# Decoder trunk (gated linear attention layer, then S5 layer): v projections of two heads issued one head earlier, gate chains of the next head issued early, q/k ahead of the output transposes

## The chip, the cores and the metric

One core of a Trainium2 chip. The metric is the device time of one execution in microseconds; the time of the kernel before is the median of three runs.

## What is computed

A sequence of 512 tokens of width 1024 goes through two layers and a final RMSNorm. The change lies in the first, gated linear attention (GLA):

```python
h = rmsnorm(x, gla_norm)
q, k, v, z, r = split(h @ w_in)                 # q, k: 4 heads x 128; v, z: 4 heads x 512; r: 16
log_a = log_sigmoid(r @ w_gate_up + b_gate) / 16
# per head, in chunks: bcum = cumsum(log_a) in the chunk
att = tril((q * exp(bcum)) @ (k * exp(-bcum)).T)
o   = att @ v + (q * exp(bcum)) @ state         # state: decayed sum of k_end.T @ v over chunks before
o   = rmsnorm_per_head(o) * head_gain * silu(z)
x   = x + o @ w_out
```

The second layer is an S5 state space layer (`u` and `z` projections, a grouped complex-diagonal scan, a GLU with a 2048x2048 matrix, an output projection). Its tables (powers of the diagonal, products with B and C) depend on parameters alone. This kernel computes them beside the first layer.

## The kernel before, in words

**Matmuls.** Every dense product is made of three fp32r matmuls (`three`, L194): high times high, high times low, low times high. A weight unit (`wunit`, L178) is one 512 KB DMA from the SP queue, a cast on ScalarE (ACT, L161) for the high part and a subtraction on VectorE (DVE, L162) for the low part. For `w_out` the unit is scaled, in two halves, on ACT (L164) and DVE (L165). A projection for one head (`dense_tok`, L204) takes four such units. It adds into four PSUM tiles of the pool `pd`, which has four in all, one for each 128 tokens; they come free when the projection's evacuation has read them. With `late` the evacuation of the last unit comes after the generator's last yield.

**A head** (loop at L634). `gate(h)` (L425): a small matmul (L427) into a tile of the pool `pt` (two tiles), then a chain of ACT and DVE operations (L429 to L451) that ends in the factors `eq` and `ek`. `proj_qk` (L454): two weight units into two `po` tiles, evacuated by multiplying with `eq` and `ek` (L465, L466). `ptrn(0..3)`: the transposes (`turn`, L399, L406) of the gated output of the head before, each into a `pt` tile. Then `weave` (L541) walks through a list of projections and, at each yield ("slot"), issues the attention pieces whose position in `POS` is that slot: `scores` (c, L485, a `pt` tile), `state` (s, L499) and `mix` (x, L515) of the four 128-token blocks. `proj_v` (L381) evacuates v into eight `big` tiles (L164, L165), which s and x read. `proj_z` (L389) evacuates z into the gate of the head's output (L393, L394, L396) and needs the norm that ends with x3. `proj_out(h - 1)` (L534) adds the product of the head before with `w_out` to x (L537).

The slots before: head 0 has z only (4 slots), since its v is made ahead of the loop; heads 1 and 2 have v, out of the head before, z (12 slots); head 3 has v, half of out, z (10 slots) and then the other half of out beside its own transposes.

**S5 tables.** `tick` issues the six parts of `small` (L968), some 200 small DVE and GpSimd (POOL) operations with a round trip through DRAM; its fourth part and its fifth use `pt` tiles for transposes (L1179, L1192; L1222, evacuated by L1224). After that `hook` issues steps of a plan: F (`compute`, L1282, on POOL, and `finish_b`, L1318), Z (`finish_z`, L1323, with eight matmuls L1330 into a `pt` tile), E (`etab`, L1247, the first three on DVE, the others on POOL). Each hook adds `RATES[head]` (0.84 in heads 1 and 2, 0.88 in head 3) to a counter, and each whole number issues a step. Before, hooks begin in head 1: two after q/k (`QZ[0]`) and one a slot.

**Order.** The order that instructions are issued in gives each a priority; `later(n)` moves a block behind by n (attention pieces by `SCP` = -20, so ahead; `small` by `LOW1` = 20). The framework's planner then orders each engine's queue by priority and by what it expects to be ready, so a projection can stand ahead of pieces that were issued before it but wait. Each engine works through its queue in that order.

```python
        if h == 0:
            weave([z], tk)
            prep.zero()
            tick()
        elif h < NH - 1:
            weave([proj_v(h, *v), proj_out(h - 1, prev, range(2)), z], tk)
```

Of the kernel before, what the change touches and what calls it, by code (L numbers as in the profile page):

```python
# [24 lines left out]
NT = SEQ // P  # L25
DI = 2048
NH = 4
# [21 lines left out]
SU = 11  # L49
SS = 22  # L50
SE = 3
WR, WH, Q4, BIG = 2, 5, 9, 28
TOFF = 5
SMALL = [0, 1, 3, 4, 5]
NPRE = 3
TS = [2, 3, 3, 3, 4, 5, 5, 5, 6, 6, 7, 8, 10, 10, 11, 12]
# [3 lines left out]
SCP = -20  # L60
USP = 50
SEQ0 = 'h0 u h2 u h4 u s h6 u x0 t x1 q0 q1 t'
GP = 4
RATES = [0.84, 0.84, 0.88, 0.94, 0.94]
LOWS = {'F': 0, 'Z': 20, 'E': 100, 'G': 0}
ETABS = [2, 3, 3, 3, 3, 3, 3, 3, 4, 4, 4, 4, 4, 4, 4, 7, 8]
POS = [[0, 0, 1, 2, 1, 2, 3, 1, 2, 3, 3], [0, 1, 1, 3, 4, 5, 6, 5, 5, 7, 9], [0, 1, 3, 4, 4, 5, 6, 5, 6, 8, 8], [1,
    1, 4, 4, 4, 5, 6, 6, 6, 6, 8], [0, 0, 0, 0]]
A0S = [3, 4, 5, 6, 7, 8, 9, 10, 11, 12, 13, 14, 15, 16, 17, 18]
SRS = [2, 3, 4, 5, 6, 7, 8, 9, 10, 11, 12, 13, 14, 15, 16, 17]  # L70
# [5 lines left out]
LBS = [0, 0, 0, 6, 7, 7, 8, 9, 10, 11, 12, 13, 14, 15, 16, 18]  # L76
UNITP = [0, 1, 0, 1, 1, 1, 0, 1, 1, 1, 0, 1, 1, 0, 1, 1, 1, 1, 1, 0, 0, 1, 1, 1, 1, 1, 0, 1, 0, 0, 1, 0, 0, 0, 0, 0,
    0, 0, 1, 1]
TORD = ['c0 c1 s0 c2 x0 s1 x1 c3 s2 x2 x3', 'c0 c1 c2 c3 x0 s0 s1 x1 s2 x2 x3', 'c0 c1 c2 c3 s0 x0 s1 s2 x1 x2 x3',
    'c0 c1 c2 c3 s0 s1 x0 x1 s2 x2 x3']  # L80
PACE = [2, 2, 2, 2, 2, 2, 3, 1, 2, 2, 2, 2, 2, 2, 2, 2, 2, 2, 1, 1, 1, 1]
QZ = [2, 3]
GPOS = [0, 0, 7]


def f(t):
# [4 lines left out]
def trunk_kernel(  # L91
# [5 lines left out]
    nc = tc.nc  # L97
# [20 lines left out]
    def PT():  # L118
        return PS_("pt", 2)
# [10 lines left out]
    def q2(dt=F32, n=512):  # L130
        return T_([P, n], "q2", 8, dt)

    def big(dt=F32):
        return T_([P, 512], "big", BIG, dt)
# [4 lines left out]
    def tmp(dt=F32):  # L139
        return T_([P, 512], "tmp", 4, dt)  # L140
# [18 lines left out]
    def split(dst_hi, dst_lo, src, scale=None, E=V):  # L159
        if scale is None:  # L160
            i0 = A.copy(out=dst_hi, in_=src)  # L161
            i1 = E.tensor_tensor(out=dst_lo, in0=src, in1=f(dst_hi), op=SUB)  # L162
        else:
            i0 = A.activation(out=dst_hi, in_=src, func=AF.Copy, scale=scale)  # L164
            i1 = V.scalar_tensor_tensor(out=dst_lo, in0=src, scalar=scale, in1=f(dst_hi), op0=MUL, op1=SUB)  # L165
        return i0.ins, i1.ins
# [214 lines left out]
    def proj_v(h, vh, vl):  # L381
        vh += [big(F32R) for _ in range(NT)]
        vl += [big(F32R) for _ in range(NT)]

        def ev(tb, acc):
            split(vh[tb], vl[tb], acc, scale=rs1[:, tb:tb + 1])
        return dense_tok(w_v[h], hh, hl, ev)
# [11 lines left out]
    def turn(box, out_):  # L399
        oh, ol = out_  # L400

        def fn(tb):
            o2 = box[0][tb]
            pt = PT()
            for k in range(4):
                PE.transpose(pt[:, k * P:(k + 1) * P], o2[:, k * P:(k + 1) * P], ident)  # L406
            oh.append(q2(F32R))
            ol.append(q2(F32R))
            split(oh[tb], ol[tb], pt)
        return fn  # L410
# [14 lines left out]
    def gate(h):  # L425
        lg = PT()
        PE.matmul(lg, lhsT=wg[:, h * P:(h + 1) * P], rhs=rT, start=True, stop=True)  # L427
        mn = tmp()
        V.tensor_scalar(out=mn, in0=lg, scalar1=bg[:, h:h + 1], scalar2=0.0, op0=ADD, op1=ALU.min)  # L429
        ab = tmp()  # L430
        A.activation(out=ab, in_=lg, func=AF.Abs, bias=bg[:, h:h + 1])
        A.activation(out=ab, in_=ab, func=AF.Exp, scale=-1.0)
        A.activation(out=ab, in_=ab, func=AF.Ln, bias=1.0)
        V.tensor_tensor(out=mn, in0=mn, in1=ab, op=SUB)
        be = tmp().rearrange("p (b c) -> p b c", b=NT)
        V.tensor_tensor_scan(out=be.rearrange("p b c -> p (b c)"), data0=seg.rearrange("p b c -> p (b c)"),
                             data1=mn, initial=0.0, op0=MUL, op1=ADD)
        sm = T_([P, 3, NT], "gsm", 2)
        V.tensor_copy(out=sm[:, 0, :], in_=be[:, :, 63])
        V.tensor_copy(out=sm[:, 1, :], in_=be[:, :, 127])  # L440
        V.tensor_tensor(out=sm[:, 2, :], in0=sm[:, 1, :], in1=sm[:, 0, :], op=SUB)
        V.tensor_tensor(out=be, in0=be, in1=sm[:, 0, :].unsqueeze(2).to_broadcast([P, NT, P]), op=SUB)
        es = T_([P, 3, NT], "ges", 2)
        A.activation(out=es, in_=sm, func=AF.Exp, scale=1.0 / 16)
        eq = big()
        ek = big()
        b2 = be.rearrange("p b c -> p (b c)")
        A.activation(out=eq, in_=b2, func=AF.Exp, scale=1.0 / 16)
        A.activation(out=ek, in_=b2, func=AF.Exp, scale=-1.0 / 16)
        V.tensor_tensor(out=eq, in0=eq, in1=rbc, op=MUL)  # L450
        V.tensor_tensor(out=ek, in0=ek, in1=rbc, op=MUL)  # L451
        return es, eq, ek
# [81 lines left out]
    def proj_out(h, o, ns):  # L534
        for n in ns:
            def ev(tb, acc, n=n):
                V.tensor_tensor(out=xts[tb][n], in0=acc, in1=xts[tb][n], op=ADD)  # L537
            yield from dense_tok(w_out[h, n], o[0], o[1], ev, per_tb=True,
                                 scales=[hgp[:, k:k + 1] for k in range(4)])

    def weave(gens, toks):  # L541
        i = 0
        for gen in gens:
            for _ in gen:
                with later(SCP):
                    for p, fn, b in toks:
                        if p == i:
                            fn(b)
                if prep.t < TOFF:
                    if i % 2:  # L550
                        tick()
                else:
                    hook()
                i += 1

    def toks(h, at_):
        fns = {"c": at_.scores, "s": at_.state, "x": at_.mix}
        off = {"c": 0, "s": 4, "x": 7}
        return [(POS[h][off[t[0]] + int(t[1])], fns[t[0]], int(t[1])) for t in TORD[h].split()]

# [37 lines left out]
    v0 = ([], [])  # L598
# [32 lines left out]

    prev = ptrn = None
    nxt = []
    for h in range(NH):  # L634
        v = ([], [])
        box = []
        o = ([], [])
        trn = turn(box, o)
        if h == 0:
            v = v0  # L640
            proj_r()
        phase[0] = h - 1 if h else 0
        gt = nxt.pop() if nxt else gate(h)
        if h > 0:
            ptrn(0)
            ptrn(1)
        qk = proj_qk(h, gt[1], gt[2])
        if h > 0:
            ptrn(2)
            ptrn(3)  # L650
        if h == 0:
            tick()
        else:
            for _ in range(QZ[0]):
                hook()
        at_ = Attn(gt[0], qk, v, box)
        z = proj_z(h, box)
        tk = toks(h, at_)
        if h < 3 and GP >> h & 1:
            tk.append((GPOS[h], lambda b: nxt.append(gate(b)), h + 1))  # L660
        if h == 0:
            weave([z], tk)
            prep.zero()
            tick()
        elif h < NH - 1:
            weave([proj_v(h, *v), proj_out(h - 1, prev, range(2)), z], tk)
        else:
            weave([proj_v(h, *v), proj_out(h - 1, prev, range(1)), z], tk)
            weave([proj_out(h - 1, prev, (1,))], [(POS[4][b], trn, b) for b in range(4)])
            load_a(0)  # L670
            load_b(0)
        prev, ptrn = o, trn
# [754 lines left out]
```

## Time and profile before

| | us |
|---|---|
| median of 3 runs (1067.58 to 1072.58) | 1069.05 |
| the profiled execution | 1069.13 |
| its span, first to last instruction | 1067.4 |
| around the span | 1.7 |
| PE (TensorE matmul) busy | 939.7 (88%) |
| DVE busy | 745.0 (70%) |
| ACT busy | 431.8 (40%) |
| POOL busy | 519.5 (49%) |

The GLA layer takes the span up to about 523 us and the S5 layer the rest. The shares are averages over both. Heads can be told apart by the gate matmul L427, which is the only one with the form 16*128.

### The profile page before, as it was taken

Reading aid. Unit: us, or ns where it says so; the run is one execution under the profiler, and the core shown is the slowest. Engines: PE = TensorE matmul, PEld = TensorE weight load, DVE = VectorE, ACT = ScalarE, POOL = GpSimd, SP = SyncE. Lnnn points to the kernel's source line nnn. Section 1 sums busy time; section 2 is a strip of 40 time slices with the busy share of each in tenths; the row PEclk is TensorE's granted clock in tenths of the full one; section 3 lists DMA queues with packets and bytes.
Section 4 is the critical chain, followed back from the end, with each engine's and each line's share of the span. In section 5 each row is a group of like instructions: output and inputs, shape, how many; then the busy total and the mean of one; then the engine's idle time right before and its main releaser. Section 6 shows DMA issues by size and latency. Waiting matters only on the chain. (4 is left out here: it accounts for less than half of the span.)

```text
span 1067.4 us, 13596 instructions
## 1 busy us (share of the span) xinstructions
PE 939.7 (88%) x5019; PEld 726.8 (68%) x5019; DVE 745.0 (70%) x920; ACT 431.8 (40%) x639; POOL 519.5 (49%) x441
## 2 busy tenths in 40 slices
PE   6996955898888979889799998998999999999996
PEld 5674833666656756567667776786877888888884
DVE  4896579968999779978427769698996432324323
ACT  5332243325345234343375663643353432313212
POOL 3037747699898899997643335263314000000000
PEclk9996976998989989899989999998999999999998
DMA  8521275596576786697844457586764322362232
GB/s 258 153 95 29 74 220 174 175 260 199 158 221 202 209 251 203 200 317 251 258 151 148 144 188 231 191 284 226 256 218 129 114 84 98 99 177 82 97 99 79
DMA packets 113522, 186.91 MB, mean 175 GB/s; under 512 B 31824, under 2 KB 69248, under 8 KB 113456
## 3 DMA queue, kind: packets, MB, share of 16 engines
q1 hardware_dynamic: 110208, 180.90, 54.7%
q10 hardware_dynamic: 2960, 4.99, 1.3%
q8 instruction: 39, 0.64, 0.2%
q14 instruction: 27, 0.22, 0.1%
q0 software_dynamic: 288, 0.15, 0.1%
HBM read 148.81 MB, written 45.59 MB: 182 GB/s over the span
## 5 line engine op out<-in xcount | busy, mean ns | idle before, releaser
L162 DVE TENSOR_TENSOR whl<-wraw,whl 128x1024 fp32r<-128x1024 f32 x97 | 134.2, 1384 | 171.1 <-PE pt L197 45.4
L161 ACT CAST whl<-wraw 128x1024 fp32r<-128x1024 f32 x120 | 125.9, 1049 | 287.0 <-PE pd L202 48.5
L200 PE MATMUL pd<-whl,actA 128*128 128x512 f32 x384 | 154.8, 421 | 28.9 <-ACT whl L161 16.8
L201 PE MATMUL pd<-whl,actA 128*128 128x512 f32 x384 | 160.5, 418 | 5.9 <-DVE whl L162 5.9
L202 PE MATMUL pd<-whl,actA 128*128 128x512 f32 x384 | 157.6, 412 | 0.0
L268 POOL TENSOR_TENSOR rstd<-rv,neghalf 128x1 f32<-128x1 f32 (+1 forms) x6 | 4.7, 788 | 247.0 <-DVE rv L267 247.0
L200 PEld LDWEIGHTS pd<-whl,actA 128*128 128x128 f32 x384 | 76.5, 200 | 53.7 <-ACT whl L161 18.1
L196 PE MATMUL pd<-actA,whl 128*128 128x512 f32 x256 | 102.4, 409 | 4.5 <-ACT u L729 4.1
L198 PE MATMUL pd<-actA,whl 128*128 128x512 f32 x256 | 100.8, 399 | 0.0
L201 PEld LDWEIGHTS pd<-whl,actA 128*128 128x128 f32 x384 | 77.0, 200 | 26.7 <-DVE whl L162 8.1
L202 PEld LDWEIGHTS pd<-whl,actA 128*128 128x128 f32 x384 | 76.9, 201 | 17.5 <-issue 0.8
L162 POOL TENSOR_TENSOR whl<-wraw,whl 128x1024 fp32r<-128x1024 f32 x23 | 59.0, 2570 | 61.3 <-PE pd L202 19.3
L200 PE MATMUL pd<-whl,q 128*128 128x512 f32 x192 | 77.7, 411 | 5.8 <-DVE tmp L394 3.0
L201 PE MATMUL pd<-whl,q 128*128 128x512 f32 x192 | 77.1, 403 | 0.8 <-DVE whl L165 0.7
L1315 DVE TENSOR_TENSOR q<-q,q 128x1024 f16<-128x1024 f32 x32 | 60.0, 1876 | 15.4 <-ACT q L1314 13.1
L1290 POOL TENSOR_TENSOR q<-q,q 128x1024 f32<-128x1024 f32 x16 | 47.3, 2958 | 33.7 <-DMA q<-s_bi 20.2
L809 POOL TENSOR_TENSOR tmp<-xx,q 128x512 f32<-128x512 f32 x13 | 23.8, 1834 | 79.7 <-DVE xx L807 64.5
L196 PEld LDWEIGHTS pd<-actA,whl 128*128 128x128 f32 x256 | 48.9, 191 | 17.9 <-ACT u L729 6.0
L198 PEld LDWEIGHTS pd<-actA,whl 128*128 128x128 f32 x256 | 49.0, 192 | 11.6
L1314 ACT CAST q<-q 128x1024 f16<-128x1024 f32 x32 | 33.2, 1041 | 55.2 <-POOL q L1293 38.2
L196 PE MATMUL po<-actA,whl 128*128 128x512 f32 x128 | 51.9, 406 | 4.1 <-ACT big L525 4.1
L197 PE MATMUL pd<-actA,whl 128*128 128x512 f32 x128 | 51.7, 404 | 0.0
(331 smaller groups left out, 2394.2 us busy)
## 6 DMA issues: line engine op xcount, KB each, us to landing
wraw<-w_glu SPq DMA_DIRECT2D x32, 512.0 KB, 3.4
wraw<-w_v SPq DMA_DIRECT2D x16, 512.0 KB, 5.9
wraw<-w_z SPq DMA_DIRECT2D x16, 512.0 KB, 3.4
q<-lpt SPq DMA_DIRECT2D x16, 512.0 KB, 5.2
q<-s_bi SPq DMA_DIRECT2D x16, 512.0 KB, 6.4
wraw<-w_out SPq DMA_DIRECT2D x16, 512.0 KB, 4.5
bmd<-q SPq DMA_DIRECT2D x16, 512.0 KB, 3.7
tab<-q SPq DMA_DIRECT2D x32, 256.0 KB, 4.3
```

The source lines that it names most:

```text
L161: i0 = A.copy(out=dst_hi, in_=src)
L162: i1 = E.tensor_tensor(out=dst_lo, in0=src, in1=f(dst_hi), op=SUB)
L196: PE.matmul(acc, lhsT=wh, rhs=ah, start=first, stop=False)
L197: PE.matmul(acc, lhsT=wh, rhs=al, start=False, stop=False)
L198: mark["pe"] = PE.matmul(acc, lhsT=wl, rhs=ah, start=False, stop=last).ins
L200: PE.matmul(acc, lhsT=ah, rhs=wh, start=first, stop=False)
L201: PE.matmul(acc, lhsT=ah, rhs=wl, start=False, stop=False)
L202: mark["pe"] = PE.matmul(acc, lhsT=al, rhs=wh, start=False, stop=last).ins
L809: G.tensor_tensor(out=t1, in0=sh, in1=co, op=MUL)
L1290: tt(out=m, in0=lp, in1=bb, op=MUL)
L1314: nc.scalar.copy(out=hl[:, 0], in_=src)
L1315: nc.vector.tensor_tensor(out=hl[:, 1], in0=src, in1=hl[:, 0], op=SUB)
```

## The change

In the loop over heads:

- `proj_v(1)` goes into head 0's slots, ahead of z (8 slots in place of 4); `proj_v(2)` goes into head 1's slots, behind `out(0)` and ahead of z; head 2 has out and z alone (8 slots in place of 12); head 3 keeps its own v.
- The gates of heads 1, 2 and 3 are all issued in the head before, at slots 5, 9 and 6 (`GP` = 7, a bit for each head; before, only head 3's was, at slot 7 of head 2).
- `proj_qk` is issued ahead of all four output transposes of the head before (before: between the second and the third).
- The positions and the order of the attention pieces in heads 0 and 2 (`POS`, `TORD`) are fitted to eight slots.
- `BIG`, the number of `big` tiles, is 34 in place of 28; the room comes from a smaller DMA scratch (`dynamic_dma_scratch_size=4096`).
- `TOFF` is 6: in head 0 the odd slots 1, 3 and 5 issue ticks and slots 6 and 7 are hooks.

```diff
-WR, WH, Q4, BIG = 2, 5, 9, 28
-TOFF = 5
+WR, WH, Q4, BIG = 2, 5, 9, 34
+TOFF = 6
...
-GP = 4
+GP = 7
...
-POS = [[0, 0, 1, 2, 1, 2, 3, 1, 2, 3, 3], [0, 1, 1, 3, 4, 5, 6, 5, 5, 7, 9], [0, 1, 3, 4, 4, 5, 6, 5, 6, 8, 8], [1,
+POS = [[0, 0, 1, 3, 1, 2, 4, 1, 3, 4, 6], [0, 1, 1, 3, 4, 5, 6, 5, 5, 7, 9], [0, 0, 1, 3, 1, 2, 4, 1, 3, 4, 6], [1,
...
-GPOS = [0, 0, 7]
+GPOS = [5, 9, 6]
...
+    vs = {0: v0}
     for h in range(NH):
-        v = ([], [])
...
+        v = vs.pop(h) if h in vs else ([], [])
         if h == 0:
-            v = v0
             proj_r()
...
-        if h > 0:
-            ptrn(0)
-            ptrn(1)
         qk = proj_qk(h, gt[1], gt[2])
         if h > 0:
-            ptrn(2)
-            ptrn(3)
+            for b in range(NT):
+                ptrn(b)
...
+        if h < 2:
+            vs[h + 1] = ([], [])
         if h == 0:
-            weave([z], tk)
+            weave([proj_v(1, *vs[1]), z], tk)
             prep.zero()
             tick()
-        elif h < NH - 1:
-            weave([proj_v(h, *v), proj_out(h - 1, prev, range(2)), z], tk)
+        elif h == 1:
+            weave([proj_out(0, prev, range(2)), proj_v(2, *vs[2]), z], tk)
+        elif h == 2:
+            weave([proj_out(1, prev, range(2)), z], tk)
...
-    nc = bacc.Bacc("TRN2", target_bir_lowering=False, num_devices=1)
+    nc = bacc.Bacc("TRN2", target_bir_lowering=False, num_devices=1, dynamic_dma_scratch_size=4096)
```

## Rows read from the trace of the kernel before

**Rows 1.** Stretches of the span. Columns: the stretch and its length, then for each engine its busy time and the number of its instructions, the granted TensorE clock, the DMA share and GB/s.
```profile
30.00:77.00 47.00, 45.57 (x198) 33.57 (x197) 42.77 (x118) 20.43 (x31) 7.08 (x18) 1.00 0.37 120
77.00:97.00 20.00, 14.28 (x45) 8.51 (x44) 19.50 (x48) 6.18 (x13) 17.74 (x28) 0.74 0.15 48
97.00:150.00 53.00, 36.88 (x163) 28.97 (x163) 25.86 (x36) 16.20 (x27) 27.69 (x33) 0.86 0.40 107
150.00:240.00 90.00, 69.29 (x267) 50.06 (x268) 80.54 (x82) 28.29 (x46) 74.80 (x52) 0.86 0.69 204
240.00:300.00 60.00, 48.06 (x208) 35.26 (x207) 56.33 (x57) 28.44 (x43) 53.86 (x41) 0.88 0.60 186
300.00:360.00 60.00, 56.97 (x238) 42.59 (x238) 55.67 (x52) 25.11 (x39) 55.76 (x44) 0.98 0.66 198
360.00:430.00 70.00, 57.92 (x256) 42.59 (x256) 60.94 (x57) 25.70 (x38) 65.52 (x48) 0.93 0.75 231
430.00:523.00 93.00, 83.13 (x370) 63.67 (x369) 81.44 (x80) 40.46 (x72) 85.65 (x72) 0.94 0.83 256
523.00:573.00 50.00, 42.21 (x215) 32.09 (x214) 13.31 (x24) 24.32 (x32) 15.50 (x13) 0.90 0.57 177
```

**Rows 2.** The timeline of PE between 100 and 180 us, the instructions ahead of which it stood idle longest. Columns: start, duration, line, operation; in brackets the idle time before it and what ended that.
```profile
101.06 0.80 PE L196 MATMUL po<-actA,whl 128*128 128x512 f32 x1 [4.09 <-ACT big L525]
147.39 0.77 PE L489 MATMUL pt<-big,big 128*128 128x128 f32 x2 [8.90 <-DVE big L466]
149.94 2.07 PE L200 MATMUL pd<-whl,actA 128*128 128x512 f32 x4 [0.93 <-ACT whl L161]
164.38 0.80 PE L489 MATMUL pt<-big,big 128*128 128x128 f32 x2 [5.44 <-DVE big L162]
171.17 1.22 PE L200 MATMUL po<-big,big 128*128 128x512 f32 x2 [5.99 <-ACT big L164]
176.55 0.80 PE L200 MATMUL pd<-whl,q 128*128 128x512 f32 x1 [2.12 <-DVE big L165]
```

**Rows 3.** The timeline of PE, users of `pt` tiles in turn: the table part's transposes (L1192, L1222), scores of head 0 (L489), the gate of head 1 (L427), the first transposes of head 0's output (L406).
```profile
92.09 0.43 PE L1192 MATMUL pt<-ident,tmp 64*128 64x64 f32 x2
92.45 0.49 PE L489 MATMUL pt<-big,big 128*128 128x128 f32 x2
122.27 1.04 PE L1222 MATMUL pt<-ident,q 128*64 128x128 f32 x8
127.95 1.03 PE L1222 MATMUL pt<-ident,q 128*64 128x128 f32 x8
132.81 1.12 PE L427 MATMUL pt<-u 16*128 16x512 f32 x2
133.86 0.66 PE L406 MATMUL pt<-ident,big 128*128 128x128 f32 x4
```

**Rows 4.** The timeline of DVE between 97 and 150 us, instructions ahead of which it stood idle, and the evacuation that ends head 1's gate chain (L466).
```profile
96.46 0.75 DVE L174 SCALAR_TENSOR_TENSOR big<-big,ges,big 128x512 fp32r<-128x512 f32 x1
108.92 0.29 DVE L267 TENSOR_SCALAR rv<-ssq 128x4 f32<-128x4 f32 x1 [11.71 <-ACT tmp L272]
128.59 1.28 DVE L1224 COPY q<-pt 64x512 f32<-64x512 f32 x2 [4.40 <-PE pt L1222]
133.97 0.75 DVE L429 TENSOR_SCALAR tmp<-pt,bg 128x512 f32<-128x512 f32 x1 [4.10 <-PE pt L427]
146.56 0.68 DVE L466 TENSOR_TENSOR big<-po,big 128x512 f32<-128x512 f32 x1
149.92 1.23 DVE L162 TENSOR_TENSOR whl<-wraw,whl 128x1024 fp32r<-128x1024 f32 x1 [2.68 <-ACT whl L161]
```

**Rows 5.** The timeline of POOL: the table part's operations (L990), the first operation of the first F step (L1290) and the last long one of the last F step (L1301).
```profile
69.75 0.34 POOL L990 TENSOR_TENSOR q<-big,q 128x64 f32<-128x64 f32 x1 [33.12 <-DVE q L1009]
...
102.24 0.21 POOL L1339 TENSOR_TENSOR dk<-dm,kd 128x16 f32<-128x16 f32 x1 [6.09 <-DMA kd<-kdd]
...
107.92 1.26 POOL L990 TENSOR_TENSOR q<-big,q 128x256 f32<-128x256 f32 x2
...
111.10 2.32 POOL L990 TENSOR_TENSOR q<-big,q 128x256 f32<-128x256 f32 x2
...
123.56 1.29 POOL L990 TENSOR_TENSOR q<-q,q 128x512 f32<-128x512 f32 x1
...
147.69 2.35 POOL L1290 TENSOR_TENSOR q<-q,q 128x1024 f32<-128x1024 f32 x1 [18.89 <-DMA q<-s_bi]
...
486.96 1.93 POOL L1301 TENSOR_TENSOR q<-big,pp 128x1024 f32<-128x1024 f32 x1
```

**Rows 6.** Groups of DVE instructions by line and form, from 30 to 70 us. Columns: line, operation, out<-in, form and count, busy time in all, mean ns of one, idle time before them.
```profile
L162 DVE TENSOR_TENSOR whl<-wraw,whl 128x1024 fp32r<-128x1024 f32 x6 | 7.3, 1215 | 0.4 <-ACT whl L161 0.4
L165 DVE SCALAR_TENSOR_TENSOR big<-pd,rstd,big 128x512 fp32r<-128x512 f32 x4 | 3.0, 747 | 0.2 <-ACT big L164 0.2
```

**Rows 7.** The same view from 180 to 300 us.
```profile
L1315 DVE TENSOR_TENSOR q<-q,q 128x1024 f16<-128x1024 f32 x12 | 21.9, 1835 | 8.0 <-ACT q L1314 8.0
L162 DVE TENSOR_TENSOR whl<-wraw,whl 128x1024 fp32r<-128x1024 f32 x10 | 17.0, 1698 | 0.6 <-ACT whl L161 0.6
L1320 DVE TENSOR_TENSOR q<-q,q 128x1024 f32<-128x1024 f32 x6 | 13.0, 2158 | 0.0
```

**Rows 8.** Who waited for whom, ACT from 78 to 500 us. Columns: the waiting line and what it waited for, us in all, times, the longest.
```profile
ACT q L1314 <- POOL q L1293: 38.2, 8, 9.6
```

**Rows 9.** The timeline of PE at the head of head 2: its gate matmul, and the first scores.
```profile
242.06 1.12 PE L427 MATMUL pt<-u 16*128 16x512 f32 x2
...
283.33 0.49 PE L489 MATMUL pt<-big,big 128*128 128x128 f32 x2 [0.20 <-DVE q L162]
```

More of the change, by code (lines that the diff above doesn't have):

```diff
@@ L78 @@
     0, 0, 1, 1]
-TORD = ['c0 c1 s0 c2 x0 s1 x1 c3 s2 x2 x3', 'c0 c1 c2 c3 x0 s0 s1 x1 s2 x2 x3', 'c0 c1 c2 c3 s0 x0 s1 s2 x1 x2 x3',
+TORD = ['c0 c1 s0 c2 x0 s1 x1 c3 s2 x2 x3', 'c0 c1 c2 c3 x0 s0 s1 x1 s2 x2 x3', 'c0 c1 s0 c2 x0 s1 x1 c3 s2 x2 x3',
     'c0 c1 c2 c3 s0 s1 x0 x1 s2 x2 x3']
```

## The prediction

> **What bounds the kernel now.** I first read the busy times by stretches [rows 1], since the page's shares average two layers with different limits. From 150 to 523 us, heads 1 to 3, DVE is busy 335 of 373 us and POOL 336, while PE has 315 and its clock stands between 0.86 and 0.98. So the layer is not held by PE there. DVE has hardly any room, and POOL none to speak of. From 97 to 150 us it is the reverse: DVE is busy 25.9 of 53 us, POOL 27.7, PE 36.9 at a clock of 0.86. What costs time in that stretch is not work but order, and it is the stretch that the change rearranges.
>
> I then read who is waited for at the passage from head 0 to head 1 [rows 2]. PE stands 8.9 us until k of head 1 is there (L466), 5.4 and 6.0 us between the scores and the first state, and begins `out(0)` at 176.55 only when the evacuation of v(1) frees a `pd` tile (L165). v(1) has held the four `pd` tiles since about 114 us. So v(1) was calculated early, beside the waits, but finished late, and out(0) stood behind it.
>
> The third view is the order of the `pt` tiles [rows 3]. They are handed out in the order of issue: scores c3 of head 0 run only behind the table transposes L1192, and the gate matmul of head 1 (132.81) only behind the last of the sixteen L1222 (127.95), though its operand had been ready since head 0. The transposes of head 0's output come behind it. The L1222 wait for POOL, whose table chain runs from 69.75 to about 125 us [rows 5].
>
> **The change, part by part.** The sum is made against the profiled execution, 1069.1 us (span 1067.4 and 1.7 around it); that is the median of the runs, 1069.05, to within 0.1.
>
> *A. v(1) a head earlier, gate(1) early, q/k ahead of the transposes.* No work goes away. PE, ACT and DVE do the same units, the same four DMA loads, only sooner. What can go is idle time on the engine that limits the layer, DVE: 53.0 - 25.9 = 27.1 us of it lie between 97 and 150 us [rows 1]. I go through them [rows 4]. 11.7 us end with the norm of head 0 (L267). There the weight splits of v(1) and z(0) now find room, since head 0 has twice as many slots; I count them as filled. 4.4 and 4.1 us are waits for PE transposes behind the POOL chain. By my reading of the `pt` order these stay: gate(1), issued at slot 5 of head 0, is still behind the fifth table part, issued at slot 3, so it comes at about 127 us and not much sooner. The other 6.9 us (2.7 before the weight split at 149.92, the rest in pieces inside the gate chain) are filled by the scaled weight splits of out(0), which no longer stand behind v(1). I leave 0.4 of this out as pipeline, and take 11.7 + 6.5 = 18.2 us. Bounds: 0, if the new work only piles up behind the same waits, and 27.1, if DVE is never idle.
>
> *B. v(2) in head 1, gate(2) in head 1.* The gate chain of head 2 now takes from 242.06 to the scores at 283.33 [rows 9]; in its stretch PE is idle 11.9 us but DVE only 3.7 of 60 [rows 1]. The long chain is the result of a full DVE, and an earlier start takes no DVE work away. I take 0, with 0 and 11.9 as bounds. Gate(3), one slot sooner, is 0 as well: it was issued early already.
>
> *C. Hooks.* Head 2 has four slots fewer, so 4 x 0.84 = 3.4 steps fewer, and head 0 has two hooks, 1.7 steps. Net 1.7 steps of the plan leave the layer for the S5 layer. A pair of F and Z takes DVE 2 x 1.835 + 2.158 = 5.8 us [rows 7], so 2.9 a step and 4.9 us. They land after 523 us, where DVE is busy 13.3 of 50 us [rows 1], which is the cover; without it the gain is 0. I take 4.9, bounds 0 and 4.9.
>
> *D. Price of company.* Four more weight splits of 128x1024 run in the stretch after 70 us, in which POOL is at work. Such a split takes 1.215 us beside an idle POOL [rows 6] and 1.698 beside a busy one [rows 7]: 4 x 0.48 = 1.9 us lost. The four evacuations read PSUM and take about 0.75 us [rows 6]. Bounds 0 and, if a split waits out a whole POOL operation of 2.35 us [rows 5], 9.4.
>
> The Trainium skill (SBUF — State Buffer, section "SBUF: two separate sides") says that DVE instructions with two SBUF inputs and GpSimd share one port pair under an exclusive lock, and that the loser is blocked for the whole instruction. By it D would be the 9.4 us of the upper bound, and the sum 1055 us; the trace agrees on which operations suffer, but on average shows 0.48 us a split and not a whole operation.
>
> *E. The rest.* `BIG` 34 has no price in the rows. v(1) and its gate hold ten more tiles where six were added, so the attention of head 0 has four fewer. The nearest row for a late block is the 4.1 us PE wait at 101.06 [rows 2]; I take 0, since z(0) and v(1) are there to run meanwhile, with -4.1 and +4.1 as bounds. The tick of part six moves from the end of head 0 to slot 5; F's first operation waited 18.9 us for its loads [rows 5], and I leave it where it is. The SP queue carries the same loads in another order: 0. The smaller DMA scratch touches a few small loads at the start: 0.
>
> Sum: 18.2 + 0 + 4.9 - 1.9 = 21.2 us, and 1069.1 - 21.2 = 1047.9, so **1048 us**.
>
> **Rivals.**
>
> *PE sets the pace (R1).* If the DVE work of prep gives way, the gain is what PE sees: out(0) begins as soon as the transposes of head 0's output are split, by about 142.6 us in the order of now, in place of 176.55: 34 us, so 1035. For it: PE has 58 us of idle time between 150 and 523 us [rows 1]. Against: DVE has only 38 there.
>
> *POOL sets the pace (R2).* F steps keep POOL busy from 147.69 to 486.96 without a break [rows 5], and ACT stands 38.2 us for their results, with weight casts queued behind [rows 8]. Nothing of the change starts this chain sooner. If each head is held to its share of F steps, the gain is nothing: 1069. Against: from 487 us the layer still has 36 us of its own work, so the last F step isn't what ends it.
>
> *The table chain slips (R3, slower).* Head 0 is already full on DVE between 77 and 97 us (19.5 of 20, [rows 1]), and part of that is what POOL waits for. Four splits and four evacuations ahead of it are 4 x 1.70 + 4 x 0.75 = 9.8 us of DVE work. POOL suffers too: a pair of its 128x256 operations took 1.26 us while DVE was idle (107.92) and 2.32 while it worked (111.10) [rows 5]. If both push the first F step back from 147.69 by some 8 us, and POOL paces the rest as in R2, the result is 1077. The point from which it decides: the slip of L1290's first start is larger than what head 1 saves. Against: POOL has 6.1 us of a wait for a small DMA (102.24) to swallow some of it.
>
> *Gates not early (R4).* If v(1)'s evacuation waits for `big` tiles in head 0, then `pd` stays held there, z(0) follows late and only the 6.5 us of head 1 and C are won, less D: 9.5, so 1060.
>
> **How the numbers follow.** A measurement of this kernel tells about 0.5% (5.3 us) from no change. Forecast (1040 to 1057): 0.40. R1: 0.16. R4: 0.16. R2: 0.13. R3: 0.15. Faster by over 0.5% are the forecast, R1 and R4: 0.72. Within 0.5% is R2: 0.13. Slower is R3: 0.15. The bounds of A to E added up on the good side (27.1 + 4.9 + 4.1) give 1033. A range from 1031 to 1070 leaves out R3 and a little of R1. The forecast's own range is 1040 to 1057.
>
> **What would show it right or wrong in the profile after.** A: DVE busy for more than 40 of the 53 us between 97 and 150; the first matmul of out(0) (pd<-whl,q, L200) before 150 us in place of 176.55; no wait on L465 or L466 of 8.9 us ahead of head 1's scores. The `pt` order: L427 of head 1 behind the last L1222. B: scores of head 2 within 15 us of its q/k matmuls, with DVE full all the same. C: two steps' worth of L1315, L1320 and L1330 after the layer's end. D: a mean of L162 on weight units near 1.7 us in head 0 after 70 us. R2 and R3 show in the first start of L1290 and in ACT's wait for L1293: if that wait grows by 20 us or more while the heads get no shorter, POOL paces. The forecast is wrong if DVE's idle time between 97 and 150 us comes back later as waits of DVE for ACT or POOL in heads 1 to 3, where it now has 38 us.

## The result, and the profile after

After: 1077.96 us, the median of six runs (1076.20 to 1082.64), against 1070.38 of the kernel before beside it. The ratio is 1.0066 (95% interval 1.0046 to 1.0087): slower, where 1048 was predicted, and outside the range. The profiled execution of after took 1081.8 us (span 1080.1), that of before 1069.1 (span 1067.4): 12.7 us of span to be explained, where the medians differ by 7.6. Lines behind L635 stand one higher in after (L1290 is L1291, L1222 is L1223).

The first view is the same windows as in [rows 1], for the stretches that speak. Columns: stretch, length, then busy us (x instructions) of PE, PEld, DVE, ACT and POOL, PE clock, DMA share, GB/s.

```profile
97.00:150.00 53.00, 39.29 (x156) 30.59 (x157) 21.53 (x30) 17.59 (x28) 27.38 (x34) 0.87 0.43 106
150.00:240.00 90.00, 69.18 (x282) 51.00 (x282) 80.17 (x85) 25.85 (x40) 64.54 (x45) 0.87 0.66 195
300.00:360.00 60.00, 55.51 (x243) 39.96 (x244) 47.31 (x58) 21.72 (x38) 45.80 (x46) 0.94 0.55 173
```

Part A said that DVE would be busy for more than 40 of the 53 us from 97 to 150. It is busy for 21.5, less than the 25.9 of [rows 1]: its idle time there grew from 27.1 to 31.5 us. What it waits for shows on ACT and PE. ACT's timeline in after (start, duration, line and operation; in brackets the idle time before it and what ended that):

```profile
136.79 0.69 ACT L431 ACTIVATE tmp<-pt,bg 128x512 f32<-128x512 f32 x1 [6.97 <-DVE tmp L429]
143.71 0.61 ACT L449 ACTIVATE big<-tmp 128x512 f32<-128x512 f32 x1
144.23 0.57 ACT L525 COPY big<-po 128x512 f32<-128x512 f32 x1
144.83 0.63 ACT L272 ACTIVATE tmp<-big 128x512 f32<-128x512 f32 x1
```

and PE's:

```profile
112.80 0.40 PE L202 MATMUL po<-big,big 128*128 128x512 f32 x1
121.65 0.54 PE L1223 MATMUL pt<-ident,q 128*64 128x128 f32 x3 [2.05 <-POOL q L991]
134.85 1.12 PE L427 MATMUL pt<-u 16*128 16x512 f32 x2
144.85 0.80 PE L196 MATMUL po<-actA,whl 128*128 128x512 f32 x1 [8.88 <-ACT big L525]
160.19 1.94 PE L406 MATMUL pt<-ident,big 128*128 128x128 f32 x8 [7.16 <-DVE big L396]
161.94 0.79 PE L200 MATMUL pd<-whl,q 128*128 128x512 f32 x1
```

The last attention block of head 0 (x3) leaves PE at 113.2, but ACT copies it out (L525) only at 144.23, right behind L449, the last ACT operation in the gate chain of head 1. ACT's part of that chain begins with L431 at 136.79, since the chain's matmul L427 (134.85) is behind the table transposes L1223. So x3 waited 31 us for a chain of the next head, which waited for the tables. The norm follows x3:

```profile
145.65 0.16 DVE L267 TENSOR_SCALAR rv<-ssq 128x4 f32<-128x4 f32 x1
152.24 1.24 DVE L531 TENSOR_TENSOR rsv<-rsv,rstd 128x4 f32<-128x4 f32 x1
```

L267 is at 145.65 (108.9 in before, [rows 4]), and the output transposes at 160.2 (133.9). The first F step did not slip (147.69 in [rows 5]):

```profile
147.38 2.37 POOL L1291 TENSOR_TENSOR q<-q,q 128x1024 f32<-128x1024 f32 x1 [17.36 <-DMA q<-s_bi]
```

The whole can be put on one engine. The next windows are cut where a head's norm ends (L531 of heads 0 to 3) and at the layer's end (the last L537); length minus DVE's busy time is its idle time. Before:

```profile
0.00:111.30 111.30, 90.62 (x353) 67.00 (x354) 79.49 (x194) 45.49 (x77) 43.34 (x93) 0.92 0.43 128
111.30:229.90 118.60, 85.83 (x353) 64.05 (x352) 94.56 (x108) 36.25 (x58) 84.29 (x62) 0.86 0.62 182
229.90:360.70 130.80, 115.83 (x491) 84.90 (x493) 121.55 (x114) 56.76 (x85) 120.27 (x90) 0.93 0.64 195
360.70:471.90 111.20, 92.60 (x393) 68.24 (x392) 97.08 (x87) 43.73 (x68) 105.22 (x77) 0.91 0.77 236
471.90:515.10 43.20, 39.85 (x189) 31.27 (x190) 38.31 (x43) 19.11 (x34) 37.43 (x34) 1.00 0.84 269
```

After:

```profile
0.00:152.20 152.20, 119.84 (x478) 90.36 (x479) 99.25 (x219) 60.17 (x97) 63.98 (x109) 0.92 0.47 134
152.20:254.70 102.50, 79.45 (x316) 58.16 (x315) 88.11 (x93) 31.59 (x50) 77.04 (x56) 0.87 0.65 193
254.70:360.40 105.70, 88.40 (x374) 64.44 (x373) 87.54 (x92) 40.69 (x64) 85.74 (x72) 0.90 0.59 183
360.40:482.80 122.40, 95.59 (x413) 71.56 (x411) 113.30 (x98) 51.43 (x78) 107.93 (x74) 0.91 0.71 216
482.80:529.10 46.30, 42.37 (x195) 32.60 (x196) 38.90 (x42) 18.76 (x36) 42.00 (x41) 0.91 0.84 274
```

The layer ends at 529.1 in place of 515.1, 14.0 us later; what follows takes 551.0 in place of 552.3. DVE's work up to there is 427.1 us (431.0 before), its idle time 102.0 (84.1 before): +17.9, of which head 0 has 52.9 - 31.8 = 21.1. Heads 1 and 2 are 16 and 25 us shorter, but head 0 is 41 us longer and head 3 is 11.

### The profile page after: what moved, and what is told of

It is laid out like the page before. It is cut to its first block, busy times and chain, and to the rows that moved or that the text cites. A ratio compares the mean times of both kernels' runs of the same rounds, so it can differ in the third digit from the quotient of the medians.

```text
span 1080.1 us, 13571 instructions
## 1 busy us (share of the span) xinstructions
PE 939.7 (87%) x5019; PEld 729.3 (68%) x5019; DVE 746.5 (69%) x920; ACT 432.5 (40%) x639; POOL 512.1 (47%) x441
## 5 line engine op out<-in xcount | busy, mean ns | idle before, releaser
L162 DVE TENSOR_TENSOR whl<-wraw,whl 128x1024 fp32r<-128x1024 f32 x97 | 133.1, 1372 | 165.5 <-PE pt L197 45.4
L201 PE MATMUL pd<-whl,actA 128*128 128x512 f32 x384 | 159.0, 414 | 9.5 <-DVE whl L162 9.5
L268 POOL TENSOR_TENSOR rstd<-rv,neghalf 128x1 f32<-128x1 f32 (+1 forms) x6 | 4.7, 785 | 247.9 <-DVE rv L267 247.9
L200 PEld LDWEIGHTS pd<-whl,actA 128*128 128x128 f32 x384 | 76.6, 200 | 54.1 <-ACT whl L161 9.5
L196 PE MATMUL pd<-actA,whl 128*128 128x512 f32 x256 | 102.2, 408 | 4.3 <-ACT u L730 3.2
L198 PE MATMUL pd<-actA,whl 128*128 128x512 f32 x256 | 100.7, 397 | 0.0
L201 PEld LDWEIGHTS pd<-whl,actA 128*128 128x128 f32 x384 | 76.4, 199 | 28.4 <-DVE whl L162 11.8
L200 PE MATMUL pd<-whl,q 128*128 128x512 f32 x192 | 80.0, 424 | 17.2 <-DVE tmp L394 9.2
L201 PE MATMUL pd<-whl,q 128*128 128x512 f32 x192 | 79.6, 416 | 0.3 <-DVE whl L165 0.3
L162 POOL TENSOR_TENSOR whl<-wraw,whl 128x1024 fp32r<-128x1024 f32 x23 | 59.3, 2583 | 38.8 <-ACT whl L161 17.8
L1291 POOL TENSOR_TENSOR q<-q,q 128x1024 f32<-128x1024 f32 x16 | 44.7, 2796 | 60.1 <-DMA cmd<-q 25.2
L1316 DVE TENSOR_TENSOR q<-q,q 128x1024 f16<-128x1024 f32 x32 | 58.1, 1814 | 12.6 <-ACT q L1315 12.6
L200 PEld LDWEIGHTS pd<-whl,q 128*128 128x128 f32 x192 | 38.4, 201 | 27.6 <-DVE tmp L394 9.5
L198 PEld LDWEIGHTS pd<-actA,whl 128*128 128x128 f32 x256 | 48.8, 191 | 11.6
L202 PE MATMUL pd<-whl,q 128*128 128x512 f32 x128 | 54.5, 427 | 0.0
```

Source lines behind the costliest of these rows:

```text
L196: PE.matmul(acc, lhsT=wh, rhs=ah, start=first, stop=False)
L198: mark["pe"] = PE.matmul(acc, lhsT=wl, rhs=ah, start=False, stop=last).ins
L200: PE.matmul(acc, lhsT=ah, rhs=wh, start=first, stop=False)
L201: PE.matmul(acc, lhsT=ah, rhs=wl, start=False, stop=False)
L202: mark["pe"] = PE.matmul(acc, lhsT=al, rhs=wh, start=False, stop=last).ins
L268: G.tensor_tensor(out=dst, in0=v, in1=neghalf.to_broadcast([P, w]), op=ALU.pow)
```

## The experiments

Each kernel was timed beside the kernel before; a ratio stands to that. Medians are of 4 to 10 executions. "Idle" is DVE's idle time up to the layer's end, and "slot 6" the kernel of the first experiment. The diffs are against after unless another kernel is named.

**1. gate(1) one slot later, behind x3.**

```diff
-GPOS = [5, 9, 6]
+GPOS = [6, 9, 6]
```

> The changed kernel with one number changed: gate(1) is issued at slot 6 of head 0, behind x3, in place of slot 5, ahead of it. T1 (x3's copy of o gets its place and its tile behind the gate chain of head 1, and that chain waits for the table transposes): the norm of head 0 (L267) at about 115 us in place of 145.6, the first output transpose about 130 in place of 160, and 5 to 25 us less than the changed kernel, so 1053 to 1073. T2 (v(1) loads DVE so much in head 0 that the table chain and everything behind it slip): L267 may move, but the first F step stays at 147 and the time stays at 1078. T3 (four hooks fewer in head 2 starve POOL, and the loss is made there and in head 3): the time stays within 4 us of 1078.

1064.77 us, ratio 0.9927 (0.9902 to 0.9952). One slot of one gate chain turns slower into faster, by some 13 us against after. DVE and ACT in this kernel:

```profile
120.14 0.83 DVE L267 TENSOR_SCALAR rv<-ssq 128x4 f32<-128x4 f32 x1 [3.33 <-ACT tmp L272]
```
```profile
118.78 0.58 ACT L525 COPY big<-po 128x512 f32<-128x512 f32 x1
136.96 0.69 ACT L431 ACTIVATE tmp<-pt,bg 128x512 f32<-128x512 f32 x1 [7.05 <-DVE tmp L429]
```

The gate chain itself begins on ACT as in after (136.79). Idle is 86.8. One part of T1 missed: the first output transpose comes at 144.53 and not at about 130, since the gate chain now stands ahead of it (L441 is a step of that chain):

```profile
144.53 0.63 PE L406 MATMUL pt<-ident,big 128*128 128x128 f32 x4 [2.70 <-DVE gsm L441]
```

**2. No early gate(1), and gate(1) at slot 3.**

```diff
-GP = 7                 # first kernel
+GP = 6
-GPOS = [5, 9, 6]       # second kernel
+GPOS = [3, 9, 6]
```

> The changed kernel with GP = 6: gate(1) is not issued early but at the start of head 1, as in the kernel before; all else as changed. T1: the same gain as with slot 6, 1053 to 1073, since again nothing of the gate stands ahead of x3. T2 and T3: 1078, or later by what the early gate was worth.

> The changed kernel with gate(1) at slot 3 of head 0: by the queue order it now stands ahead of the sixteen table transposes for its pt tile, but ahead of x2 and x3 as well. T1: the harm is not being ahead of x3 but being behind the transposes at the same time; here the chain ends by about 110 us, head 1's scores start before 140, and the time is the best of the four, 1045 to 1068. T2: the gate chain's 5 us of DVE work come on top of a full DVE, so 1078 or more. T3: 1074 to 1080.

Without: 1073.74, ratio 1.0010 (0.9993 to 1.0026); L267 at 122.1. So x3 is as free as at slot 6, but less than half of slot 6's gain over after is there: T1's "same gain" is a miss, and the early gate chain, behind x3, is worth the rest, some 9 us. At slot 3: 1079.95, ratio 1.0064 (1.0044 to 1.0085), a miss for T1; T2's number came, but not by DVE work. There the gate matmul came at 99.75, ahead of the tables, but the chain then stood on ACT ahead of v(1)'s evacuation, and PE waited for that (PE's timeline):

```profile
113.62 0.79 PE L200 MATMUL pd<-whl,actA 128*128 128x512 f32 x1 [11.79 <-DVE big L165]
```

L267 came at 133.7. At slots 3 and 5 the early gate chain costs by what stands behind it; only the thing behind it changes.

**3. More steps of the plan in head 2.** The rival was that the four hooks taken from head 2 starve POOL.

```diff
-RATES = [0.84, 0.84, 0.88, 0.94, 0.94]
+RATES = [0.84, 1.176, 0.88, 0.94, 0.94]
```

> The changed kernel with the step rate of head 2 raised from 0.84 to 1.176, so that its ten hooks issue as many plan steps (11.8) as fourteen did before; nothing in head 0. T3: POOL, busy 45.8 of the 60 us from 300 to 360 in the changed kernel, is busy over 54, and the time falls to 1066 to 1071. T1 and T2: within 4 us of 1078, since the loss is in head 0.

1091.35, ratio 1.0170 (1.0136 to 1.0204): T3 is refuted. T1 and T2 missed the time too: it is 13 us above 1078. From 300 to 360 POOL is busy 54.1 us, but head 2 grows from 105.7 to 124.2 while head 3 only shrinks from 122.4 to 113.9.

**4. eq and ek of the gate chain from a pool of their own, at slot 5.**

```diff
-WR, WH, Q4, BIG = 2, 5, 9, 34
+WR, WH, Q4, BIG = 2, 5, 9, 30
-        eq = big()
-        ek = big()
+        eq = T_([P, 512], "gk", 4)
+        ek = T_([P, 512], "gk", 4)
```

> The changed kernel with gate(1) left at slot 5, but the gate's factors eq and ek in four tiles of a pool of their own; big has 30 tiles in place of 34, so the memory is the same. T1a (the order in which the pool big hands out its tiles is what puts x3's copy behind the gate): x3's copy of o no longer follows the gate chain, L267 of head 0 at 115 to 122 us, and the time as with slot 6, 1060 to 1072. T1b (x3 is late by its place in the order alone, or because there are too few big tiles): L267 stays at 145 and the time at 1078 or, with four tiles fewer, more.

1072.26, ratio 0.9997 (0.9970 to 1.0023). ACT in this kernel:

```profile
118.87 0.57 ACT L525 COPY big<-po 128x512 f32<-128x512 f32 x1
136.40 0.69 ACT L431 ACTIVATE tmp<-pt,bg 128x512 f32<-128x512 f32 x1 [7.05 <-DVE tmp L429]
139.60 0.62 ACT L272 ACTIVATE tmp<-big 128x512 f32<-128x512 f32 x1
```

The copy is free, at 118.87; the square behind it still waits, since its junk output is a `tmp` tile and the gate chain's `tmp` tiles were handed out ahead of it (experiment 5 tests this). So T1a is half right: L267 comes at 141.59, only 4 us sooner than in after. The first transposes come at 146.03, 14 us sooner, and the time is some 6 to 7 us better.

**5. The junk of the square from its own pool too**, so that nothing of x3 shares a tile order with the gate chain (against kernel 4).

```diff
-WR, WH, Q4, BIG = 2, 5, 9, 30
+WR, WH, Q4, BIG = 2, 5, 9, 29
-        junk = tmp()
+        junk = T_([P, 512], "junk", 1)
```

> The changed kernel with its gate(1) left at slot 5, but eq and ek of the gate chain taken from a pool of their own (as in the last experiment with own tiles) and now also the junk output of the square L272 from a pool of its own, so that nothing of x3 of head 0 shares a tile order with the gate chain. T1 (x3 stands behind the gate chain through the order of the two pools, and through nothing else): copy L525 and square L272 of x3 both run before 122, norm L267 at about 120 (145.65 in the changed kernel, 141.6 with eq and ek alone moved), first transposes L406 at about 144, and the time as with the gate at slot 6: 1060 to 1068. Rival (something of slot 5 other than the tiles holds head 0, for instance the order on DVE or PE): L267 stays at 138 or later and the time at about 1072.

Head 0 did as T1 said: transposes at 144.7 and L267 at 114.67, right behind the square:

```profile
114.67 0.17 DVE L267 TENSOR_SCALAR rv<-ssq 128x4 f32<-128x4 f32 x1 [2.56 <-ACT junk L272]
```

The order in which the two pools hand out tiles is what held x3. The time did not follow: 1083.05, ratio 1.0098 (1.0069 to 1.0126). The same windows as above, for this kernel:

```profile
0.00:121.50 121.50, 99.94 (x406) 75.90 (x406) 82.98 (x196) 49.16 (x80) 49.31 (x98) 0.96 0.44 130
121.50:250.30 128.80, 102.34 (x401) 73.70 (x401) 103.81 (x114) 44.23 (x68) 91.28 (x68) 0.87 0.65 188
250.30:360.30 110.00, 88.27 (x353) 62.84 (x354) 92.08 (x92) 39.41 (x62) 85.65 (x71) 0.86 0.57 177
360.30:483.00 122.70, 97.89 (x416) 73.28 (x414) 109.12 (x99) 50.82 (x76) 108.16 (x75) 0.89 0.74 220
483.00:529.80 46.80, 42.78 (x198) 32.89 (x199) 37.18 (x42) 20.20 (x38) 42.99 (x41) 0.91 0.80 258
```

Against after, idle in head 0 fell from 52.9 to 38.5, and in heads 1 to 3 it rose from 41.7 to 56.5. What was saved in head 0 came back as other waits. At slot 6 it did not (head 0 42.1, heads 1 to 3 38.8; the first three windows):

```profile
0.00:126.40 126.40, 102.69 (x414) 77.82 (x415) 84.31 (x198) 48.68 (x80) 55.13 (x101) 0.95 0.43 125
126.40:254.30 127.90, 99.38 (x403) 72.25 (x402) 111.93 (x122) 47.69 (x72) 91.44 (x68) 0.90 0.68 195
254.30:351.40 97.10, 83.22 (x346) 59.33 (x346) 84.17 (x85) 35.63 (x57) 83.32 (x68) 0.90 0.63 193
```

**6. Is it the slot or the pools?**

```diff
-GPOS = [5, 9, 6]                   # first, against kernel 5
+GPOS = [6, 9, 6]
-WR, WH, Q4, BIG = 2, 5, 9, 34      # second, against slot 6
+WR, WH, Q4, BIG = 2, 5, 9, 29
-WR, WH, Q4, BIG = 2, 5, 9, 29      # third, against kernel 5
+WR, WH, Q4, BIG = 2, 5, 9, 31
-        eq = T_([P, 512], "gk", 4)
+        eq = T_([P, 512], "gk", 2)
-        ek = T_([P, 512], "gk", 4)
+        ek = T_([P, 512], "gk", 2)
```

> The kernel with both own pools (eq, ek and the square's junk; big 29) and gate(1) at slot 6 in place of 5. In both, x3 runs ahead of the gate chain, so head 0 alone can't tell them apart (norm L267 at 115 to 120). T8 (the order of issue at slot 5 or 6 costs later, in heads 1 and 2, by something other than x3): this is as fast as the gate at slot 6 without the pools, 1062 to 1070. T9 (the pools cost: 29 big tiles in place of 34 hold heads 1 and 2, and eat what head 0 gains): it stays as with both pools at slot 5, 1077 to 1085.

> The kernel with the gate at slot 6, without any pool of its own, but with 29 big tiles in place of 34. T9 (the number of big tiles holds heads 1 and 2): 1075 to 1085, and heads 1 and 2 longer than the 128 and 97 us of slot 6 with 34. T8 (the number of big tiles is no matter): 1062 to 1070, as with 34.

> Gate(1) at slot 5, both own pools, but with two tiles for eq and ek in place of four and 31 big tiles in place of 29, so that the tiles in all are as many as in the changed kernel. T9 (the size of the pools ate the gain): 1062 to 1070, L267 at about 115. T8 (slot 5 costs later in another way): 1077 to 1085, with DVE idle in heads 1 to 3 as in the run with four and 29 (57 us from the L531 of head 0 to that of head 3, where slot 6 has 39).

1081.80 (1.0087, 1.0057 to 1.0117), 1068.78 (0.9964, 0.9949 to 0.9979) and 1080.81 (1.0079, 1.0053 to 1.0106). Both theories fall: the slot is not what costs (own pools are as slow at 6), nor is the number of tiles (29 cost slot 6 little, 31 saved nothing). With both own pools the time is 16 to 18 us above slot 6, at either slot and either size.

Two things follow. With shared pools one slot is worth 1.4%; with own pools, where x3 is free at both slots, it is worth nothing that can be told (1.0098 and 1.0087). So what the slot costs goes through the shared pools, as T1 said. And the four eq and ek tiles alone did not cost this much (experiment 4, 1072.26): the three slow kernels have the junk's pool as well, which is a single tile. No run has that pool alone, or with more tiles, so it stays an untested suspect.

**7. The product of the norm on POOL.** DVE's waits from head 0's L531 on, with both own pools (what waits and for what; us in all, times, longest), and then at slot 6:

```profile
DVE rsv L531 <- POOL rsv L268: 15.3, 3, 8.0
```
```profile
DVE rsv L531 <- POOL rsv L268: 3.6, 2, 3.0
```

```diff
-                V.tensor_tensor(out=rs4, in0=rs4, in1=rs1, op=MUL)
+                G.tensor_tensor(out=rs4, in0=rs4, in1=rs1, op=MUL)
```

> The kernel with both own pools at slot 5 (29 big), with one more edit: the product rsv = rsv * rstd of a head's norm (L531, 128x4) runs on POOL, right behind POOL's pow L268, in place of DVE, so that DVE no longer stands at L531 until POOL comes to the pow. T10 (what the own pools cost is that L531 stands right behind L267 in DVE's queue: DVE waited 15.3 us there from head 0's norm on, and 3.6 with slot 6 without pools): DVE idle up to the last L537 falls by 8 or more from 104.6, and the time from 1083 to 1070 to 1075. Rival (those waits are only the place where DVE happens to wait; the time comes from elsewhere): 1079 to 1086, the idle time stands at other lines.

> The kernel with the gate at slot 6, no own pools, and the product L531 on POOL. There DVE waits only 3.6 us at L531 in the layer, so T10 gives 3 us at most: 1060 to 1066. Rival: the order of the queues shifts by the edit and the time moves by more than 5 us either way.

On kernel 5: 1076.10, ratio 1.0045 (1.0026 to 1.0065), some 6 us better, about a third of what was to be explained. But idle fell only from 104.6 to 101.9; DVE's busy time fell more, from 425.2 to 419.7. So T10 is not confirmed as the mechanism, and the rest of what the own pools cost is open. On slot 6: 1065.67, ratio 0.9957 (0.9938 to 0.9975), no different from slot 6 alone.

**8. The parts of the change, at slot 6.** The plan rate of head 3 lowered; v(2) back in head 2, with the attention places for 8 and 12 slots and gate(2) at slot 6 (not shown in the diff); q/k back between the transposes.

```diff
-RATES = [0.84, 0.84, 0.88, 0.94, 0.94]      # first
+RATES = [0.84, 0.84, 0.70, 0.94, 0.94]
-            weave([proj_out(0, prev, range(2)), proj_v(2, *vs[2]), z], tk)   # second
+            weave([proj_out(0, prev, range(2)), z], tk)
...
+            weave([proj_v(2, *v), proj_out(1, prev, range(2)), z], tk)       # h == 2
+            ptrn(0); ptrn(1)                # third, ahead of proj_qk
-            for b in range(NT):
-                ptrn(b)
+            ptrn(2); ptrn(3)                # behind it
```

> Gate(1) at slot 6, and the step rate of head 3 lowered from 0.88 to 0.70, so that 2.5 plan steps go from head 3 into the S5 layer. T4 (each head lasts as long as the F and Z steps that are issued in it, about 9 us of POOL a step): head 3, 122 us from norm to norm with slot 6, falls by 12 to 22 us, and the time by 5 to 15 us, less what the later tables cost the S5 layer. T5 (head 3 is held by its own work on DVE, and the steps only fill gaps): head 3 falls by at most 2.5 x 2.9 = 7 us, and the time changes by under 4 us.

> Gate(1) at slot 6, v(1) moved into head 0, but v(2) back at the head of head 2, so head 1 has 8 slots and head 2 has 12, with the attention positions for those numbers and gate(2) at slot 6 of head 1. T4 (steps pace the heads): head 1 has 3.4 steps fewer and falls by 20 us or more, head 2 grows by as much; the time is within 5 us of slot 6. T5: head 1 gains only the DVE work of v(2), some 10 us, and loses the cover for the wait on out(0); 3 to 12 us slower than slot 6.

> Gate(1) at slot 6, q/k again between the second and the third output transpose, all else as changed. Both theories: q/k matmuls run ahead of the transposes by the planner's order in either case, so within 3 us of slot 6. If the new place is what delays the transposes (the first at 144.5 us with slot 6, 133.9 before), they come 5 us or more sooner here and the time falls by 3 to 8 us.

Head 3 fell from 122.4 to 110.8 us, but the part behind its norm grew from 592.6 to 599.9; 1063.79, ratio 0.9922 (0.9893 to 0.9952), as slot 6. The 11.6 us lie between what T5 and T4 allowed; what leaves the layer is in good part paid back behind it. v(2) back: 1073.36, ratio 1.0006 (0.9988 to 1.0024), so its move, with its places and gate(2), brought some 8 us at slot 6. q/k back: 1069.48, ratio 0.9966 (0.9948 to 0.9985), its interval touching that of slot 6: the order of q/k and transposes can't be told from nothing.

**9. The other side: before, with parts of the change.** The first keeps both v at home, with `TOFF` and the attention places of before (not shown in the diff), and has the early gates, q/k order and pool of the change; the second is before with the early gate(1) alone.

```diff
-            weave([proj_v(1, *vs[1]), z], tk)      # first, against slot 6 with v(2) back
+            weave([z], tk)
-            weave([proj_out(0, prev, range(2)), z], tk)
+            weave([proj_v(1, *v), proj_out(0, prev, range(2)), z], tk)
...
-GPOS = [6, 6, 7]
+GPOS = [3, 9, 7]
```
```diff
-GP = 4                 # second, against before
+GP = 5
-GPOS = [0, 0, 7]
+GPOS = [3, 0, 7]
```

> All of the change but the two moves of v: v(1) and v(2) are projected in their own heads as before, the gate chains of heads 1 to 3 are issued early (gate(1) at the last slot of head 0, behind x3), q/k stand ahead of the output transposes, more big tiles. Against the run with v(1) alone moved (1073.4) it prices the move of v(1). Theory of the prediction (moving v(1) fills idle DVE time of head 0 and frees pd for out(0)): this one is slower than 1073, about 1078 to 1085. Rival T6 (v(1) in head 0 only lengthens head 0 by what head 1 saves: norm L267 119 in place of 109, scores of head 1 18 us later): 1068 to 1074, with L267 at about 109 and the scores of head 1 at about 148.

> The kernel before with one thing added: the gate of head 1 is issued at the last slot of head 0 (behind x3). Nothing else of the change is in it. Theory of the prediction (part A counts an early gate(1) as worth little, since it stays behind the table transposes): 1067 to 1071, L427 at 131 to 133. Rival: the gate chain, now ahead of the division L393 on ACT, holds the output of head 0 as x3 was held in the changed kernel: 1073 to 1078. Second rival: the gate chain off the passage helps the scores of head 1 by 3 us or more and the time falls below 1066.

1082.06, ratio 1.0083 (1.0057 to 1.0110), and 1077.18, ratio 1.0044 (1.0026 to 1.0063). In the second the gate matmul runs at 98.4, ahead of the table transposes, and x3 is not held (L267 at 113.2). The rival named what is held instead: L393 of head 0, behind the gate chain on ACT; its range (1073 to 1078) holds the 1077.18. In before all four L393 run from 108.79 on without a wait; here the last one is at 125.64, and it waits for DVE as well:

```profile
125.64 0.69 ACT L393 ACTIVATE tmp<-pd,hrs 128x512 f32<-128x512 f32 x1 [2.18 <-DVE big L396]
```

Behind that comes a part that no theory named. DVE's queue is full with the late output of head 0 (L394, L396) and the gate chain (L450, L451) when the first table transposes are done (L1222 at 127.49), so their evacuation L1224 comes 13 us later than in before; 5 of these are the transposes' own delay (122.27 in before). DVE in this kernel, and in before:

```profile
136.37 0.67 DVE L1224 COPY q<-pt 64x512 f32<-64x512 f32 x1
```
```profile
122.91 1.28 DVE L1224 COPY q<-pt 64x512 f32<-64x512 f32 x2 [0.36 <-PE pt L1222]
```

The zero block that the tables need (L960, a memset into a `tmp` tile) is late too: it is issued behind the gate and stands behind its chain, at 128.41 in place of 117.68. POOL in this kernel:

```profile
128.41 0.19 POOL L960 MEMSET tmp<- 128x112 f32 x1 [1.86 <-ACT big L449]
163.83 2.34 POOL L1290 TENSOR_TENSOR q<-q,q 128x1024 f32<-128x1024 f32 x1 [27.92 <-DMA q<-s_bi]
```

F's load `s_bi` is issued by SP behind the stores of the tables (`lpt`, `pw`) and of the zero block (`kz`). SP in this kernel, and in before:

```profile
137.07 11.64 SPq L1227 DMA_DIRECT2D lpt<-q  x16
151.78 4.28 SPq L963 DMA_DIRECT2D kz<-tmp  x7
156.79 0.59 SPq L1275 DMA_DIRECT2D q<-s_bi  x1
```
```profile
124.50 5.22 SPq L1227 DMA_DIRECT2D lpt<-q  x8
137.63 1.87 SPq L963 DMA_DIRECT2D kz<-tmp  x2
140.23 0.60 SPq L1275 DMA_DIRECT2D q<-s_bi  x1
```

The stores of the tables begin 12.6 us later, and the zero block's stores ahead of the load take 2.4 us more. The first F step slipped by 16 us (147.69 in [rows 5]), and the layer's end by 9.5 (524.6 for 515.1); no run tells what of this is the slip and what is the late output of head 0 (its transposes come at 147.95 in place of 133.86). In the first of the two F starts at 162.2 as well. So the first kernel does not price the move of v(1): its number is what the prediction's theory gave, for another reason. The move of v(1) by itself stays unpriced.

## Why the prediction was wrong

**The step that failed is A**, and in two places.

*The order.* A argued that gate(1), issued at slot 5, stays behind the fifth table part in the order of `pt`. That was right (L427 at 134.85, 132.81 before, [rows 3]). It did not go one step on: x3 is issued at slot 6, behind gate(1), and takes its `big` and `tmp` tiles from the same pools in order of issue. What waits for the tables is then not only gate(1) but all that is behind it, the last block of head 0 first. The prediction named the question (what is late next) for PE and DVE but asked it only of `pt`, and E priced the `big` pool by its number of tiles, not by its order. Experiments 1, 4 and 5 show both links, `big` for the copy and `tmp` for the square. What the slot costs is 1.4% (experiments 1 and 6). "About 127" for gate(1) was also optimistic by 8 us.

*The premise.* Even with x3 free, the idle time of DVE from 97 to 150 isn't filled. The same window at slot 6:

```profile
97.00:150.00 53.00, 44.51 (x189) 33.80 (x187) 26.36 (x39) 17.71 (x28) 27.18 (x34) 0.95 0.36 86
```

DVE is busy 26.4 us (25.9 before), but PE 44.5 in place of 36.9. v(1) brought head 0 12 us of PE work (90.6 to 102.7 up to L531), and part of DVE's waits became waits for PE: 6.7 of its 26.6 idle us are weight splits for tiles that PE still reads (`DVE whl L162 <- PE pd L201` in the view of waits), where before 11.7 us stood ahead of L267. Another 6.4 us stand ahead of L165 (the view names no releaser), the low half of v(1)'s evacuation: its high half (L164) now stands on ACT behind a DMA issue that waits for its source, 8.66 us at slot 6 (the last section shows the same in after). "No work goes away" was right, and so 18.2 of the 27.1 idle us could not be counted before asking which engine, or which queue, would set that stretch. The rest goes in waits of under 4 us each. At slot 6 the layer ends at 518.1, with DVE busy 431.3 and idle 86.8: the sums of before (431.0 and 84.1). In its profiled execution (1068.1, which is 3.3 above its median) slot 6 gains only behind the layer, 548.3 for 552.3.

**B** (0 for v(2)): experiment 8 gives it some 8 us at slot 6, inside its bounds of 0 and 11.9. The sign that B named isn't there: in after the scores of head 2 begin 24 us behind its last q/k matmul, not within 15. In after head 2 is 25 us shorter, but head 3 is 11 us longer. It has six F and six Z steps as before. New on DVE in its stretch are the gate chain of head 3, two scaled splits of `w_out` and two L1316. Gate(3), which B took as early in both, has its matmul at 357.73 in after, just ahead of the norm of head 2, and at 318.65 in before.

**C** (4.9 us from steps that leave the layer): two L1316 do start behind the layer's end in after (529.3 and 547.0). No run has these steps alone. The nearest is experiment 8: 2.5 steps fewer in head 3 saved 11.6 us there and cost 7.3 later, and the medians show no gain (1063.79 for 1064.77). So the cover that was counted on took only part of it.

**D** (-1.9): not seen. From 70 to 150 us there are seven splits in place of six, not four more, and they take 1319 ns each, less than the six of before (1610). The estimate of 9.4 us that the prediction made by the port rule of the Trainium skill (SBUF — State Buffer, "SBUF: two separate sides") is further off still.

**E** (0 for `big`, for the tick, for the scratch): the number of `big` tiles is worth some 4 us at slot 6 (34 to 29 in experiment 6; the two intervals touch). Its order was worth a stall of 31 us.

**The rivals.** R3 gave 1077, and 1078 came, but its mechanism is absent: L1291 begins at 147.38, 0.3 us before its time in before. That number was right by chance. A slip of that kind does occur in experiment 9, where 16 us of it, together with a late output of head 0, went with some 5 us of time (0.44%). R1 (PE sees the gain) fails with A: out(0) did begin earlier, at 161.94 for 176.55, and nothing came of it. R2 fails too: ACT's wait for L1294 (L1293 before) is 26.9 us, less than the 38.2 of [rows 8]. R2 also read POOL as busy from 147.69 to 486.96 "without a break"; it is busy 307.7 of those 339.3 us. R4 (v(1)'s evacuation held by `big` tiles, 1060) has the right victim: the evacuation was held, but by ACT's DMA issue. The 1033 of the added bounds leaves out the 11.9 of B; with it they give 1021. The falsifier that the prediction named, DVE's idle time of head 0 coming back as waits in heads 1 to 3, is what experiment 5 shows, 15 us against after. Why it stays away at slot 6 and not with own pools is open; about a third of the difference goes with L531.

## What to carry to other kernels

Where pools hand out tiles in order of issue, moving a chain ahead of something puts that something behind everything the chain waits for; look for it in each pool that both use, `pt`, `big` and `tmp` here, and move the chain behind the last block that must not wait. Idle time of the busiest engine is a gain only if no other engine, and no queue, sets that stretch once the work is there. A stall removed in one stage must be followed to the end: count the idle time by stage up to the layer's end before and after, not in the one stage.

## What the runs showed that was not expected

One slot in the place of one gate chain is worth 1.4% (ratio 0.9927 for 1.0066), and freeing the same block by two own pools gains nothing, though the block ran earlier still; what those pools cost is open. A DMA that was issued from ACT's queue and waited for its source held ACT: 6.73 us ahead of 101.47 in after (the ACT operation behind the issue of `etac`, here v(1)'s evacuation):

```profile
100.79 0.63 ACTq L699 DMA_DIRECT2D etac<-etd  x1
101.47 0.69 ACT L164 ACTIVATE big<-pd,rstd 128x512 fp32r<-128x512 f32 x1 [6.73 <-DMA etd<-tmp]
```

And a norm of four columns cost DVE a wait of 8 us in experiment 5 (L267 at 241.63, L531 at 250.32), since its `pow` (L268) stood in POOL's queue behind F work until 249.26.
